# Low-rank products on zero-padded full tiles, among the first heads' values; the input normalised by 512 columns

## The chip, the cores and the metric

The kernel runs on one NeuronCore of one Trainium2 chip. The metric is the device time of one execution in microseconds (us), lower is better. Before the change three runs gave 1459.98, 1460.8 and 1462.34 us; their median is 1460.8 us. One further execution was profiled.

The engines of the core are named as in the profile: PE is TensorE (matrix products and transposes), PEld its weight loads, DVE is VectorE, ACT is ScalarE, POOL is GpSimd, SP issues most of the loads. Each engine works through its own list of instructions in order, and waits where an operand, a buffer or a weight is not ready.

## The reference, cut to what matters

One decoder layer on 272 tokens (16 meta tokens and 256 of the input) of width 2048, in float32:

```python
h = layer_norm(concat([meta, x]), emb_ln_g, emb_ln_b)        # 272 x 2048
p = h @ w_in                                                 # all projections at once
p = p + (p_prev - p) * mu                                    # RWKV columns: shift by one token
r, k, v, wl, al, gl = split(p)                               # 1024, 1024, 1024, 64, 64, 160
w_log = -softplus(-(w0 + tanh(wl) @ w2)) - 0.5               # low rank, 64 -> 1024
a = sigmoid(a0 + al @ a2)                                    # low rank, 64 -> 1024
g = sigmoid(gl) @ g2
... RWKV-7 recurrence per head of 64, stick-breaking attention per head of 64,
... output projection, layer norm, gated MLP of width 5632 with a width-3 convolution, layer norm
```

## The kernel before, in words

**Arithmetic.** A float32 operand is split in two float32r halves, high and low, and a product of two split operands is three PE passes: high x high, high x low, low x high (`passes`, lines 226 to 230, and `each_pass`, lines 493 to 500, in the same order). The tokens are the moving operand (272 or 260 columns), 128 rows of weights are the stationary one. Projecting 2048 input features to 128 output features of one kind for one pair of heads is 16 blocks of the contraction (`KT`) times 3 passes, 48 passes.

**Weights.** `weight(i)` (lines 161 to 189) issues the load of piece i and of a few ahead on SP's queue. ACT copies the piece to the high half (`whi`, or `xhi` for the first 12 pieces), DVE subtracts to get the low half (`wlo`, `xlo`; POOL does it for the first three pieces). The first 12 pieces hold the columns of the low-rank inputs wl, al and gl in blocks of four `KT` steps. Pieces 12 and 13 are k of the first pair of heads, 14 and 15 its v, 16 and 17 its r, and so on. There are three buffers for raw pieces and three for split ones, so a split waits until PE has used an older piece.

**Prologue (lines 306 to 445).** While the input arrives, PE runs 30 idle products (`WARM`). The 272 rows of the input come as three tiles: 16 meta rows, and twice 128 rows. Their means and variances are taken; then a loop (lines 358 to 366) normalises all 2048 columns, in four slices of 512, on DVE (the 16 rows and the second 128 rows) and on ACT (the first 128 rows). Behind it stand a copy of constants and four small DVE operations on the parameters (`omu`, `ngn`, `nsb`, `omka`, lines 367 to 376). `feature_major(kt)` (lines 378 to 387) then transposes 128 columns of all three tiles on PE into one PSUM bank of four, and ACT and DVE turn that into the high and low halves of `ht[kt]`; the low half's subtraction is POOL's for odd `kt`. The loop over `kt` (lines 390 to 398) keeps `LEAD` = 2 such steps ahead, and does 9 passes each for the three groups of low-rank columns (`acc[0]` to `acc[2]`).

**Low rank (lines 400 to 443).** `lora()` shifts the three results by a token, applies tanh and splits into `sh` and `sl`; then for each of the 8 pairs of heads and each of the two matrices (w2, a2) there are two products into one bank: line 432 on all 128 rows (the high half on 64 rows, the low half of the weights against it on the other 64), and line 433 on 64 rows (high half of the weights against the low half `sl`). ACT takes the sigmoid into `sg[j]`. These run as a job beside the projection of k of the first pair (`proj(12, acc[3])`).

**Order.** Up to there a planner with a cost model orders every engine's instructions. From line 453 on, PE's order is the written one. `weave(project(...))` emits the projections pass by pass, and after every 16 passes (`SLOT`) a slot in which waiting tasks put their own products. For the first pair: v, then `rwkv_front(0)` is already begun with k, then r, then `rwkv_back(0)` is begun, then k of the second pair, and so on. `rwkv_front` (lines 575 to 610) makes a cumulative sum of `sg` (line 580), exponentials, and the square of k, and two slots later has PE sum the squares by head (`by_head`, lines 550 to 553, tile `ss`); from it come the tiles `AG` and `BK`. `rwkv_back` (lines 622 to 677) multiplies with r, and two slots later has PE form the sum named `bonus` (line 639, also through lines 552 and 553). The tiles of this stage take the memory of the prologue's, so the first ones wait for the low-rank products.

The rest (the recurrence's chain, attention, output projection, MLP) is not touched.

## Time and profile before

| | us |
|---|---|
| median of three runs | 1460.8 |
| the profiled execution | 1463.17 |
| its span from first to last instruction | 1461.4 |
| PE busy | 1359.3 (93%) |
| DVE busy | 925.5 (63%) |
| ACT busy | 723.9 (50%) |
| POOL busy | 238.9 (16%) |
| mean granted clock of PE | 0.959 |

Busy time is the time in which an engine had an instruction under way; PE's passes overlap, so the pace of a stretch is read from the starts of its passes. A granted clock of 1.00 is 2.4 GHz, of 0.50 is 1.2 GHz. Times of rows count from the start of the span.

### The profile page before, as it was taken

Reading aid. Unit: us, or ns where it says so; the run is one execution under the profiler, and the core shown is the slowest. Engines: PE = TensorE matmul, PEld = TensorE weight load, DVE = VectorE, ACT = ScalarE, POOL = GpSimd, SP = SyncE. Lnnn points to the kernel's source line nnn. Section 1 sums busy time; section 2 is a strip of 40 time slices with the busy share of each in tenths; the row PEclk is TensorE's granted clock in tenths of the full one; section 3 lists DMA queues with packets and bytes.
Section 4 is the critical chain, followed back from the end, with each engine's and each line's share of the span. In section 5 each row is a group of like instructions: output and inputs, shape, how many; then the busy total and the mean of one; then the engine's idle time right before and its main releaser. Section 6 shows DMA issues by size and latency. Waiting matters only on the chain.

```text
span 1461.4 us, 26242 instructions
## 1 busy us (share of the span) xinstructions
PE 1359.3 (93%) x10528; PEld 1267.0 (87%) x10528; DVE 925.5 (63%) x1501; ACT 723.9 (50%) x1227; POOL 238.9 (16%) x417
## 2 busy tenths in 40 slices
PE   7997898778889989897999999999999999999996
PEld 5897887677888888896899999999999998888896
DVE  7477767667867776787965555555555554444445
ACT  6654565436655664544754444444444443333331
POOL 3103664017126000064300000000000000000002
PEclk8798899879999999999999999999999999999998
DMA  7344454223444323554356556655665666666563
GB/s 232 92 127 136 107 155 106 75 70 107 125 128 107 110 84 108 150 159 145 116 183 197 183 179 187 185 186 176 187 186 180 182 187 239 193 192 196 177 199 100
DMA packets 67706, 224.10 MB, mean 153 GB/s; under 512 B 9196, under 2 KB 10932, under 8 KB 67440
## 3 DMA queue, kind: packets, MB, share of 16 engines
q1 hardware_dynamic: 63392, 215.03, 47.5%
q0 software_dynamic: 3328, 4.25, 2.2%
q10 hardware_dynamic: 864, 3.15, 0.5%
q8 instruction: 82, 1.34, 0.4%
q14 instruction: 40, 0.33, 0.1%
HBM read 219.01 MB, written 3.30 MB: 152 GB/s over the span
## 4 chain that ended last, share of the span: by engine, by line
PE 66%; DVE 10%; issue 3%; ACT 3%; DMA 2%; POOL 2%; POOLq 0%; DVEq 0%; ACTq 0%
PE u L230 11%; PE u L228 11%; PE u L229 11%; PE d L1159 5%; PE d L1158 5%; PE d L1160 5%; DVE wlo L187 3%; PE S L495 2%; PE S L499 2%; PE S L497 2%; ACT whi L184 1%; DMA dy<-Y 1%; POOL ytmp L686 1%; POOL Y L688 1%; DMA wraw<-in_w_up_dram 1%
## 5 line engine op out<-in xcount | busy, mean ns | idle before, releaser
L187 DVE TENSOR_TENSOR wlo<-wraw,whi 128x1024 fp32r<-128x1024 f32 (+1 forms) x396 | 484.8, 1230 | 371.9 <-ACT whi L184 365.5
L184 ACT CAST whi<-wraw 128x1024 fp32r<-128x1024 f32 (+1 forms) x396 | 409.1, 1040 | 505.6 <-DMA wraw<-in_w_up_dram 136.7
L228 PE MATMUL u<-h1hi,whi 128*128 128x258 f32 (+2 forms) x1408 | 400.7, 285 | 3.3 <-ACT whi L184 3.3
L230 PE MATMUL u<-h1hi,wlo 128*128 128x258 f32 (+2 forms) x1408 | 398.6, 284 | 3.3 <-DVE wlo L187 3.3
L229 PE MATMUL u<-h1lo,whi 128*128 128x258 f32 (+2 forms) x1408 | 398.6, 283 | 0.0
L230 PEld LDWEIGHTS u<-h1hi,wlo 128*128 128x128 f32 x1408 | 267.9, 190 | 4.4 <-DVE wlo L187 4.4
L228 PEld LDWEIGHTS u<-h1hi,whi 128*128 128x128 f32 x1408 | 267.8, 190 | 4.2 <-ACT whi L184 4.2
L229 PEld LDWEIGHTS u<-h1lo,whi 128*128 128x128 f32 x1408 | 267.6, 190 | 0.0
L1159 PE MATMUL d<-wlo,ahi 128*128 128x512 f32 (+1 forms) x396 | 145.7, 368 | 0.0
L1158 PE MATMUL d<-whi,ahi 128*128 128x512 f32 (+1 forms) x396 | 145.7, 368 | 0.0
L1160 PE MATMUL d<-whi,alo 128*128 128x512 f32 (+1 forms) x396 | 145.3, 367 | 0.0
L495 PE MATMUL S<-h,whi 128*128 128x272 f32 (+1 forms) x384 | 116.2, 303 | 4.0 <-DVE shr L270 2.6
L1173 POOL TENSOR_TENSOR drs<-drs,mhalf 128x1 f32<-128x1 f32 x2 | 2.1, 1036 | 717.1 <-DVE drs L1172 717.1
L499 PE MATMUL S<-h,wlo 128*128 128x272 f32 (+1 forms) x384 | 116.5, 303 | 0.0
L497 PE MATMUL S<-h,whi 128*128 128x272 f32 (+1 forms) x384 | 116.0, 302 | 0.0
L495 PE MATMUL R<-h,whi 128*128 128x272 f32 (+1 forms) x368 | 112.9, 307 | 0.0
L499 PE MATMUL R<-h,wlo 128*128 128x272 f32 (+1 forms) x368 | 112.8, 306 | 0.0
L497 PE MATMUL R<-h,whi 128*128 128x272 f32 (+1 forms) x368 | 112.0, 304 | 0.0
L1158 PEld LDWEIGHTS d<-whi,ahi 128*128 128x128 f32 x396 | 74.5, 188 | 13.1
L1160 PEld LDWEIGHTS d<-whi,alo 128*128 128x128 f32 x396 | 74.5, 188 | 13.0
L1159 PEld LDWEIGHTS d<-wlo,ahi 128*128 128x128 f32 x396 | 74.6, 188 | 12.7
L495 PEld LDWEIGHTS S<-h,whi 128*128 128x128 f32 x384 | 76.5, 199 | 6.1 <-issue 2.9
(384 smaller groups left out, 2284.7 us busy)
## 6 DMA issues: line engine op xcount, KB each, us to landing
wraw<-in_w_up_dram SPq DMA_DIRECT2D x176, 512.0 KB, 3.7
wraw<-in_w_in_dram SPq DMA_DIRECT2D x96, 512.0 KB, 3.5
wraw<-in_w_down_dram SPq DMA_DIRECT2D x88, 512.0 KB, 4.2
wraw<-in_w_out_dram SPq DMA_DIRECT2D x28, 512.0 KB, 3.5
xraw<-in_w_in_dram SPq DMA_DIRECT2D x12, 256.0 KB, 3.7
xt<-in_xin_dram SPq DMA_DIRECT2D x8, 256.0 KB, 5.1
wraw<-in_w_out_dram SPq DMA_DIRECT2D x8, 256.0 KB, 2.6
l<-in_ln_dram ACTq DMA_DIRECT2D x1, 2048.0 KB, 8.3
```

Of the source, the lines that this page charges most:

```text
L184: S.copy(hi[:, :wide], raw[:, :wide])
L187: V.tensor_sub(lo[:, :wide], raw[:, :wide], hi[:, :wide].bitcast(F32))
L228: mm(ps, lhsT=hi[:, sl], rhs=xh, start=start, stop=False)
L229: mm(ps, lhsT=hi[:, sl], rhs=xl, start=False, stop=False)
L230: mm(ps, lhsT=lo[:, sl], rhs=xh, start=False, stop=stop)
L495: mm(ps, lhsT=hi[:, sl], rhs=xh, start=start, stop=False)
L497: mm(ps, lhsT=hi[:, sl], rhs=xl, start=False, stop=False)
L499: mm(ps, lhsT=lo[:, sl], rhs=xh, start=False, stop=stop)
L686: G.tensor_tensor(out=tmp[:n_, :n, :m], in0=Y[:n_, :n, s:s + 1].to_broadcast([n_, n, m]), in1=LT[:n_, s:s + 1, s + 1:].to_broadcast([n_, n ...
L1158: mm(ps, lhsT=ahi[:, f, t_], rhs=hi[:, w], start=f == 0, stop=False)
L1159: mm(ps, lhsT=ahi[:, f, t_], rhs=lo[:, w], start=False, stop=False)
L1160: mm(ps, lhsT=alo[:, f, t_], rhs=hi[:, w], start=False, stop=f == NF - 1)
```

## The change: what it does

Low rank: `sl` becomes two tiles, each zero on the 64 rows it doesn't use, and the second product of each pair of products runs on all 128 rows. The whole of k's first half is put into the last eight steps of the loop over `kt`, its second half behind the loop. PE's written order begins there; v of the first pair is projected in this stage too, and after every 6 of its passes comes one pair of heads' low-rank products (4 of them). v leaves the woven stage, so the woven stage begins with r. Input: the normalisation is a function called for 512 columns at a time, followed by the transposes of these columns (4 `kt`), and then by their products. The copy of constants and the small operations on parameters come behind the loop. 42 idle products in place of 30.

```diff
--- before.py
+++ after.py
@@ -38,8 +38,7 @@
 MEAN = 8
 LATER = 8
 AHEAD = 300
-WARM = 30
-LEAD = 2
+WARM = 42
 CUTS = (0, 512), (512, 1088), (1088, 1664), (1664, 2048)
 LN2 = float(np.log(2.0))
 LEX, KEX = -20, 16
@@ -280,29 +279,8 @@
                     yield
 
 
...
     sg = []
+    order = ctx.enter_context(ExitStack())
     with ExitStack() as es:
         xp = pool(es, "xp")
         xw = pool(es, "xw")
@@ -311,9 +289,10 @@
         acc = [pst.tile([P, 512], F32, tag="acc", bufs=4, name=f"acc{m}") for m in range(4)]
         warm = pst.tile([P, 512], F32, tag="tr", bufs=4, name="warm")
 
-        sl = xp.tile([P, T], F32R, name="sl")
-        V.memset(sl.bitcast(F32), 0.0)
-        idle = sl.bitcast(mybir.dt.bfloat16)[:, :512]
+        sl = [xp.tile([P, T], F32R, name=f"sl{n}") for n in range(2)]
+        for t in sl:
+            V.memset(t.bitcast(F32), 0.0)
+        idle = sl[0].bitcast(mybir.dt.bfloat16)[:, :512]
         for _ in range(WARM):
             mm(warm, lhsT=idle[:, :P], rhs=idle, start=True, stop=True)
 
@@ -355,7 +334,7 @@
                 G.tensor_tensor(out=mr[:r], in0=mv[:r, 0:1], in1=rs[:r], op=ALU.mult)
                 G.tensor_scalar(out=mr[:r], in0=mr[:r], scalar1=-1.0, scalar2=None, op0=ALU.mult)
             norm.append((mv, rs, mr))
-        for k in range(4):
+        def normalise(k):
             c = slice(k * 512, k * 512 + 512)
             for (xt, r, a), (mv, rs, mr) in zip(xs, norm):
                 if a:
@@ -364,16 +343,6 @@
                                         op0=ALU.subtract, op1=ALU.mult)
                 else:
                     S.activation(xt[:r, c], xt[:r, c], AF.Identity, scale=rs[:r], bias=mr[:r])
-        S.copy(trbd, trbd_s)
-
-        omu = ap_.tile([P, 27], F32, name="omu")
-        o = PV["mu_r"][0]
-        V.tensor_scalar(out=omu, in0=pv[:, o:o + 27], scalar1=-1.0, scalar2=1.0, op0=ALU.mult, op1=ALU.add)
-        ngn, nsb = [ap_.tile([P, 8], F32, name=n) for n in ("ngn", "nsb")]
-        for t, n in ((ngn, "gn_g"), (nsb, "sb_g")):
-            V.tensor_scalar(out=t, in0=pars(n), scalar1=-1.0, scalar2=None, op0=ALU.mult)
-        omka = ap_.tile([P, 8], F32, name="omka")
-        V.tensor_scalar(out=omka, in0=pars("k_a"), scalar1=-1.0, scalar2=1.0, op0=ALU.mult, op1=ALU.add)
 
         def feature_major(kt):
             ps = pst.tile([P, 512], F32, tag="tr", bufs=4, name=f"tr{kt}")
@@ -387,15 +356,27 @@
             e.tensor_tensor(out=ht[kt][:, 1], in0=tmp, in1=ht[kt][:, 0].bitcast(F32), op=ALU.subtract)
 
 
-        for kt in range(LEAD):
-            feature_major(kt)
         for kt in range(KT):
-            if kt + LEAD < KT:
-                feature_major(kt + LEAD)
+            if kt % 4 == 0:
+                normalise(kt // 4)
+                for k in range(4):
+                    feature_major(kt + k)
             for m in range(3):
                 hi, lo = weight(kt // 4 * 3 + m, ahead=3)
                 n0 = 12 if m else 0
                 passes(acc[m][:, n0:T], hi, lo, kt % 4, ht[kt][:, 0, n0:], ht[kt][:, 1, n0:], kt == 0, kt == KT - 1)
+            if kt >= 8:
+                passes(acc[3][:, :T], *weight(12, ahead=0), kt - 8, ht[kt - 8][:, 0], ht[kt - 8][:, 1], kt == 8, False)
+        S.copy(trbd, trbd_s)
+
+        omu = ap_.tile([P, 27], F32, name="omu")
+        o = PV["mu_r"][0]
+        V.tensor_scalar(out=omu, in0=pv[:, o:o + 27], scalar1=-1.0, scalar2=1.0, op0=ALU.mult, op1=ALU.add)
+        ngn, nsb = [ap_.tile([P, 8], F32, name=n) for n in ("ngn", "nsb")]
+        for t, n in ((ngn, "gn_g"), (nsb, "sb_g")):
+            V.tensor_scalar(out=t, in0=pars(n), scalar1=-1.0, scalar2=None, op0=ALU.mult)
+        omka = ap_.tile([P, 8], F32, name="omka")
+        V.tensor_scalar(out=omka, in0=pars("k_a"), scalar1=-1.0, scalar2=1.0, op0=ALU.mult, op1=ALU.add)
 
         half = [slice(0, 64), slice(64, 128)]
         weight(11, ahead=0)
@@ -414,7 +395,7 @@
             sh = [tp_.tile([P, T], F32R, tag="tmp", bufs=2, name=f"sh{n}") for n in range(2)]
             for n, (h, o) in enumerate(zip(half, half[::-1])):
                 S.copy(sh[n][h], lw[0][h])
-                V.tensor_sub(sl[h], lw[0][h], sh[n][h].bitcast(F32))
+                V.tensor_sub(sl[n][h], lw[0][h], sh[n][h].bitcast(F32))
                 S.copy(sh[n][o], lw[0][h])
             yield
             for m in (1, 2):
@@ -430,28 +411,31 @@
                     ps = pst.tile([P, 512], F32, tag="tr", bufs=4, name=f"lora{j}{n}")
                     w = w2a2_r[:, n, j * P:j * P + P]
                     mm(ps[:, :T], lhsT=w, rhs=sh[n], start=True, stop=False)
-                    mm(ps[:, :T], lhsT=w[half[n]], rhs=sl[half[n]], start=False, stop=True)
+                    mm(ps[:, :T], lhsT=w, rhs=sl[n], start=False, stop=True)
                     S.activation(t[:, n, PAD:], ps[:, :T], AF.Sigmoid, bias=par(name, j))
                 sg.append(t)
-                if j % 2:
-                    yield
-
-        weight(12)
-        start(lora(), 1)
-        run(proj(12, acc[3]))
-        while jobs:
-            advance()
+                yield
+
+
+        order.enter_context(tc.manual_schedule(engines={PE.engine}))
+        low = lora()
+        next(low)
+        for kt in range(8, KT):
+            passes(acc[3][:, :T], *weight(13), kt - 8, ht[kt][:, 0], ht[kt][:, 1], False, kt == KT - 1)
         shift(acc[3], 8, k_[:, PAD:])
+
+        val = pst.tile([P, 512], F32, tag="acc", bufs=4, name="acc4")
+        for n, _ in enumerate(proj(14, val)):
+            next(low, None)
+        for _ in low:
+            pass
+        shift(val, 16, v_[:, PAD:])
         tc.keep_in_program_order(nc.scalar.preload_act_table_set("natural_log_exp_and_others"))
 
 
     pp = pool(astack, "pp", space=PSUM)
     ap2 = pool(astack, "ap2")
     dp = pool(astack, "dp", space=bass.MemoryType.DRAM)
-
-    order = ctx.enter_context(ExitStack())
-    order.enter_context(tc.manual_schedule(engines={PE.engine}))
-
 
 
 
@@ -878,13 +862,13 @@
     def bank(name):
         return pp.tile([P, 512], F32, tag="proj", bufs=2, name=name)
 
-    piece = 14
+    piece = 16
     state = [dict() for _ in range(NPAIR)]
     for kind, j in ORDER:
         st = state[j]
         if kind == "R":
             for n, dst in ((1, k_), (2, v_), (0, r_)):
-                if n != 1 or j:
+                if n == 0 or j:
                     ps = bank(f"R{j}{n}")
                     weave(project(piece, ps, 12 if n == 0 else 0))
                     piece += 2
```

## Rows read from the trace of the kernel before

**Rows 1.** The profile's first part (busy by engine), and one group of its fifth.
```profile
PE 1359.3 (93%) x10528; PEld 1267.0 (87%) x10528; DVE 925.5 (63%) x1501; ACT 723.9 (50%) x1227; POOL 238.9 (16%) x417
...
L187 DVE TENSOR_TENSOR wlo<-wraw,whi 128x1024 fp32r<-128x1024 f32 (+1 forms) x396 | 484.8, 1230 | 371.9 <-ACT whi L184 365.5
```

**Rows 2.** Stretches: length, busy time (instructions) by engine, granted clock, DMA share, GB/s.
```profile
10.00:20.00 10.00, 3.78 (x15) 2.41 (x15) 9.44 (x18) 6.87 (x12) 7.46 (x9) 0.72 0.61 200
20.00:30.00 10.00, 9.59 (x57) 8.62 (x58) 7.72 (x16) 5.43 (x10) 2.47 (x3) 0.76 0.74 242
...
49.00:67.40 18.40, 18.38 (x58) 12.34 (x58) 2.42 (x4) 10.11 (x22) 0.00 (x0) 0.68 0.11 36
...
60.00:70.00 10.00, 10.00 (x29) 7.07 (x30) 2.28 (x3) 5.81 (x11) 2.30 (x5) 0.50 0.00 0
```

**Rows 3.** Timeline of PE, prologue: start, length, line, operands, count [idle before].
```profile
1.20 8.13 PE L318 MATMUL warm<-sl 128*128 128x512 bf16 x30 [1.20 <-DVE sl L315]
...
20.37 0.90 PE L381 MATMUL tr<-cc,xt 16*128 16x16 f32 x3 [3.24 <-DVE tmp L384]
21.32 0.59 PE L229 MATMUL acc<-h,xhi 128*128 128x272 f32 x1
```

**Rows 4.** Timeline of DVE, then of POOL, same stretch.
```profile
13.24 5.23 DVE L363 TENSOR_SCALAR xt<-xt,mv,rs 128x512 f32<-128x512 f32 x7 [0.48 <-POOL rs L353]
...
19.77 0.54 DVE L384 TENSOR_SCALAR tmp<-tr,pv 128x272 f32<-128x272 f32 x1
...
14.61 5.00 POOL L179 TENSOR_TENSOR xlo<-xraw,xhi 128x512 fp32r<-128x512 f32 x3 [1.40 <-ACT xhi L178]
```

**Rows 5.** Groups of DVE, 13.2 to 47 us: count, busy, mean ns, idle before.
```profile
L384 DVE TENSOR_SCALAR tmp<-tr,pv 128x272 f32<-128x272 f32 x16 | 8.4, 550 | 2.6 <-ACT h L382 2.6
L179 DVE TENSOR_TENSOR xlo<-xraw,xhi 128x512 fp32r<-128x512 f32 x9 | 6.0, 693 | 0.7 <-ACT xhi L178 0.7
```

**Rows 6.** Timeline of PE at full clock: one step's transposes, and six passes apart.
```profile
31.73 0.60 PE L381 MATMUL tr<-cc,xt 16*128 16x16 f32 x3
32.08 0.37 PE L229 MATMUL acc<-h,xhi 128*128 128x272 f32 x1
...
47.88 0.29 PE L228 MATMUL acc<-h,whi 128*128 128x272 f32 x1
...
48.63 0.29 PE L228 MATMUL acc<-h,whi 128*128 128x272 f32 x1
```

**Rows 7.** Timeline of PE at full clock, low-rank products between passes of k.
```profile
57.13 0.39 PE L228 MATMUL acc<-h,whi 128*128 128x272 f32 x1
57.35 0.28 PE L432 MATMUL lora<-sh,w2a_r 128*128 128x272 f32 x1
57.57 0.39 PE L433 MATMUL lora<-sl,w2a_r 64*128 64x272 f32 x1
57.89 0.39 PE L229 MATMUL acc<-h,whi 128*128 128x272 f32 x1
```

**Rows 8.** Timeline of PE: v begins; two passes at half clock; r begins; bonus.
```profile
67.40 0.59 PE L495 MATMUL R<-h,whi 128*128 128x272 f32 x1
...
68.25 0.43 PE L495 MATMUL R<-h,whi 128*128 128x272 f32 x1
68.47 0.43 PE L497 MATMUL R<-h,whi 128*128 128x272 f32 x1
...
76.08 0.28 PE L495 MATMUL R<-h,whi 128*128 128x260 f32 x1
...
87.96 0.39 PE L552 MATMUL bonus<-ss,trbd 128*128 128x258 f32 x1 [1.92 <-ACT ss L546]
88.99 0.39 PE L553 MATMUL bonus<-sq,trbd 128*128 128x258 f32 x1 [0.65 <-DVE sq L547]
```

**Rows 9.** Timeline of DVE; then a stretch from the squares' sum to bonus.
```profile
71.30 0.46 DVE L547 TENSOR_TENSOR ss<-sq,rn 128x288 fp32r<-128x288 f32 x1 [1.45 <-ACT rn L546]
...
74.20:88.94 14.74, 12.22 (x98) 11.80 (x96) 12.34 (x22) 6.57 (x10) 0.00 (x0) 1.00 0.46 142
```

More of the change, by code (lines that the diff above doesn't have):

```diff
@@ L280, in proj @@
                     yield
-    jobs = []
-    def start(gen, wait=0, then=None):
-        jobs.append([wait, gen, then])
-    def advance():
-        for job in list(jobs):
-            if job[0]:
-                job[0] -= 1
-                continue
-            try:
-                next(job[1])
-            except StopIteration:
-                jobs.remove(job)
-                if job[2]:
-                    job[2]()
-    def run(gen):
-        for _ in gen:
-            advance()
     sg = []
+    order = ctx.enter_context(ExitStack())
     with ExitStack() as es:
@@ L432, in lora @@
                     mm(ps[:, :T], lhsT=w, rhs=sh[n], start=True, stop=False)
-                    mm(ps[:, :T], lhsT=w[half[n]], rhs=sl[half[n]], start=False, stop=True)
+                    mm(ps[:, :T], lhsT=w, rhs=sl[n], start=False, stop=True)
                     S.activation(t[:, n, PAD:], ps[:, :T], AF.Sigmoid, bias=par(name, j))
                 sg.append(t)
-                if j % 2:
-                    yield
-        weight(12)
-        start(lora(), 1)
-        run(proj(12, acc[3]))
-        while jobs:
-            advance()
-        shift(acc[3], 8, k_[:, PAD:])
+                yield
[4 more added lines that the diff above has]
+            passes(acc[3][:, :T], *weight(13), kt - 8, ht[kt][:, 0], ht[kt][:, 1], False, kt == KT - 1)
+        shift(acc[3], 8, k_[:, PAD:])
+        val = pst.tile([P, 512], F32, tag="acc", bufs=4, name="acc4")
[4 more added lines that the diff above has]
+        shift(val, 16, v_[:, PAD:])
         tc.keep_in_program_order(nc.scalar.preload_act_table_set("natural_log_exp_and_others"))
```

## The prediction

> **What bounds the kernel now.** I read the busy times first: PE has 93% of the span, no other engine more than 63% [rows 1]. So the end moves with PE, and a change in the first 90 us is worth what it takes from PE's list there, since all that follows is emitted in the same order as before. Then I read the stretches of 10 us for places where PE is idle or at a low clock. There are two. From 10 to 20 us PE is busy for 3.78 us, and the granted clock has a mean of 0.72, then 0.76 up to 30 us, while DVE is busy for 9.44 us: DVE is the bound there. From 49.0 to 67.4 us PE is always busy, but with only 58 instructions in 18.4 us; the clock has a mean of 0.68, and from 60 to 70 it is 0.50, the lower of its two levels (1.2 GHz) [rows 2]. The timelines say why. PE stops at 9.3 us, when its idle products end, and the first low-half pass starts at 21.32; the wait just ahead of it is on a DVE operation of line 384 [rows 3]. DVE couldn't do that one before 19.77, because the remaining normalising operations (seven in 5.23 us from 13.24) and the small operations on parameters stood ahead of it [rows 4].
>
> **The pace of a pass.** At full clock six passes lie between 47.88 and 48.63, 0.125 us each, and the three transposes of one step take 0.35 us (31.73 to 32.08) [rows 6]. At half clock a pass takes 0.22 us (68.25 to 68.47) [rows 8].
>
> **Part 1, the loop over `kt`.** Before, at 49.02 us, PE had done the 144 passes of the loop and 22 passes of k (48 less the 26 that the groups of the stretch from 49.0 still hold: 58 instructions less 32 low-rank ones [rows 2]). With two more, 49.3 us is what compares with the end of the new loop, which holds 144 passes and 24 of k. In the new loop DVE normalises one slice of each tile, and the first transposes follow at about 13.9 as before; but line 384 can follow them at once, not at 19.77. The work that moves costs what it did, and runs beside PE's passes. What paces the loop then? A group of four steps has on DVE 2 normalising operations at 0.75 (5.23/7 [rows 4]), 4 of line 384 at 0.55, 3 low halves of weights at 0.69 [rows 5], and two subtractions no longer than line 384's: 1.5 + 2.2 + 2.1 + 0.9 = 6.7 us. PE has 36 passes and 4 steps of transposes, 4.5 + 1.4 = 5.9 us, in the two groups without k, and 6.0 + 1.4 = 7.4 in the two with it. So DVE paces the first two groups and PE the last two: 13.24 + 2 x 6.7 + 2 x 7.4 = 41.4, and 2 us for waits at the edges of the groups, where all four transposes stand ahead of the passes: 43.5 us. Bounds: if PE has finished the first group and the second's transposes at 20 us (POOL's low halves, 14.61 to 19.61 [rows 4], allow no earlier end of it), 132 passes and 8 steps remain, 16.5 + 2.8, and the loop ends at 39.3; if DVE's order gives all back, at 49.3. I take 43.5: **5.8 us gained**, between 0 and 10.
>
> The 12 more idle products (8.13/30 = 0.27 each [rows 3]) end at 12.6, ahead of the first transposes; they cost nothing unless the input comes over 1 us earlier. They stand in the place of an idle stretch of PE after which the clock was at half. SP's loads keep their order (piece 12 is asked for earlier in the text, but still after piece 11).
>
> **Part 2, the low-rank stage.** At full clock, three instructions (a pass of k, the 128-row product, the 64-row product) take 57.13 to 57.89 = 0.76 us, where three passes in a row take 0.375 [rows 6, 7]. The two switches, to 64 rows and back, thus cost 0.385 us per pair of products, 6.2 us for 16. Of the 18.4 us of the stretch 58 x 0.125 = 7.25 are plain pace, 6.2 the switches, and the remaining 5 the half clock; and v's first passes run at half clock as well (22 of them, some 2.2 us [rows 8]). On full tiles a product is a pass like any other. After the new loop come 24 passes of k, 48 of v and 32 products: 104 x 0.125 = 13.0 us, and 0.5 for a first low-rank product that waits for tanh and the splitting (30 passes, 3.75 us, cover that; without them the wait would be all of it). Before, from 49.3 to the end of v at 76.08 [rows 8], 26.8 us went by. **13.3 us gained.** Bounds: 7.1 if a padded product still costs what the pair did (6.2 less), 13.8 without the wait. The sigmoids on ACT run beside 1.25 us of passes per pair of heads.
>
> The Trainium skill, TensorE: Matmul & The Clock Gate, section Why this matters for your kernels, says that a product with a short contraction takes the same time as a full one, and that the gain lies in running several at once. Taken alone it gives the padding nothing, and the sum is then 6.2 us smaller. The rows on 64-row products differ from that: the start after one comes 0.32 us later (57.57 to 57.89), after a full pass 0.125 [rows 6, 7]. I go by the rows.
>
> **Part 3, what is late next.** v's 48 passes lay between `rwkv_front(0)` and `rwkv_back(0)` and gave DVE and ACT time for the front. They are gone from there, and so PE comes to `bonus` earlier, relative to the front. Before, 76.08 to 88.99 = 12.9 us lay between the start of r and bonus' second product, the last of them a wait [rows 8]. After: the front can begin at the end of the low-rank products (its tiles lie in their memory). In the trace the squares' low half was ready 71.30 + 0.46 - 67.40 = 4.4 us after that point [rows 8, 9]; with the product itself 5.0. From there to bonus DVE's list took 14.74 us [rows 9]. In it were five low halves of weights at 1.2 (mean in [rows 1]) and v's shift, 0.5; with half as many passes beside it, three of the five fall out: 14.7 - 3.6 - 0.5 = 10.6. Together 15.6 us, against PE's own list of 48 + 32 + 2 passes, 10.2 us: PE waits over 5 us at bonus, where it now waits some 3. Also, r may start in the PSUM bank in which v stood and wait a microsecond for v's shift; that wait lies inside the 15.6. Bounds: 10.2, if DVE's order favours the chain, and 21.6 (67.40 to 88.99), if nothing gets shorter. **2.7 us lost.**
>
> **The sum.** 5.8 + 13.3 - 2.7 = 16.4 us less: bonus at 72.6 instead of 88.99. Behind it PE's order, the weights and the slots are the same (48 passes are three whole slots), so the shift stays. The profiled execution gives 1463.2 - 16.4 = 1446.8; it lies 2.4 above the median of the runs, so the median becomes **1444.4 us**.
>
> **Rivals.**
> - *Padding saves the clock, not the switches.* The price of a low-rank pair stays 0.385 us more: 1450.6 us. For it: the skill's sentence above. Against it: rows 7. Chance 0.08.
> - *The low-rank stage stays at half clock,* for a reason other than the 64-row products. For it: the clock was at half for most of the 18.4 us though PE was always busy. Against it: plain passes just ahead ran at 0.125. 80 instructions x 0.1 = 8 us: 1452.4. Chance 0.06.
> - *DVE gives it back.* The loop ends at 49.3 and the front takes its 21.6: 16.4 - 5.8 - 6.0 = 4.6 gained, 1456.2. For it: DVE was busy for 9.4 of 10 us [rows 2], and keeps all its work. Chance 0.06.
> - *The grouped transposes let the clock fall in the loop: slower.* Four steps of transposes in a row, and a wait behind them at each edge of a group, replace single steps between passes. If the clock then stays at half over the loop, 168 passes at 0.22 and 16 steps at 0.7 make 48 us, from about 14.5 to 63, 20 us more than forecast: 1464. It decides when over four fifths of the loop run at half clock. For it: between 10 and 30 us, with transposes and few passes, the clock was at half for about 10 us (means 0.72 and 0.76 [rows 2]). Against it: PE was then idle, and in the loop 36 or 48 passes follow every group. Chance 0.06.
>
> The Trainium skill, TensorE: Matmul & The Clock Gate, Part 4: PE-mode transpose, says that transposes don't count as busy for the clock in the way that products do. That is the rule behind the fourth rival; by it the sum would be 1464. The trace so far doesn't settle it, since transposes and idle time came together.
>
> **How the numbers follow.** The forecast's own case (a loop that ends between 39 and 47 us, a front between 11 and 18) has 0.70 and gives 1438 to 1451. With the first two rivals 0.84 lies up to 1454; so the range is 1438 to 1454. The remaining 0.04 is no visible change (a different planning of ACT and DVE in the woven stage that costs what the start gains). A change of under 0.2%, 2.9 us, can't be told from none. Faster: forecast and first three rivals, less a little, 0.88; same 0.05; slower 0.07.
>
> **What would show it.** Right: the loop's last pass at about 43.5; low-rank products 0.125 us apart with a granted clock of 1.00; r's first pass near 57; a longer wait at bonus, whose second product stands near 72.6; and the same distance from there to the end as before. Wrong: a granted clock of 0.5 in the loop; PE waiting for a low half of weights or of `h` for several us; a wait at bonus beyond 8 us; or a stretch behind 100 us that has become longer.

## The result and the profile after

| | before | after |
|---|---|---|
| median of 12 runs each, us | 1460.4 | 1451.53 |
| ratio, 95% interval | | 0.9944 [0.9926, 0.9961] |
| the profiled execution, us | 1463.17 | 1458.17 |
| its span, us | 1461.4 | 1456.4 |
| mean granted clock | 0.959 | 0.958 |
| PE / DVE busy, us | 1359.3 / 925.5 | 1359.0 / 927.4 |

The change gains 8.9 us of 1460 (by the interval of the ratio, 5.7 to 10.8). The forecast was a gain of 16.4 us (1444.4 us), the range 1438 to 1454. Both the sign and the range hold; about half of the forecast's gain did not come. Three marks on PE's timeline show where:

| mark, us from the span's start | before | forecast | after |
|---|---|---|---|
| loop done (144 passes, and 24 of k) | 49.3 | 43.5 | 47.9 |
| k, v and low-rank products done | 76.1 | 57.0 | 61.4 |
| bonus' second product | 88.99 | 72.6 | 78.93 |

The middle stage is as forecast (13.5 us from 47.9 to 61.4). The loop before it and the front behind it are each too long, by 4.4 and 1.9 us. (The 49.3 of before is the prediction's count and holds the 0.26 us in which the first low-rank product waited. Counted as in the later table, by passes alone, before's loop is done at 49.0; the loop then gains 1.1 us and the stage 13.6.)

The stretches of after, to be read beside [rows 2] (length, busy time of PE, PEld, DVE, ACT and POOL with instructions, granted clock, DMA share, GB/s):

```profile
10.00:20.00 10.00, 7.54 (x30) 4.26 (x27) 9.46 (x18) 7.53 (x14) 7.23 (x9) 0.71 0.55 181
20.00:30.00 10.00, 9.29 (x60) 8.93 (x61) 8.51 (x15) 5.96 (x10) 4.18 (x5) 0.78 0.91 306
...
47.90:61.40 13.50, 13.49 (x106) 13.13 (x104) 6.68 (x11) 12.81 (x30) 0.00 (x0) 1.00 0.35 123
...
61.40:78.90 17.50, 12.35 (x85) 11.77 (x83) 11.15 (x21) 10.34 (x19) 2.30 (x5) 0.90 0.33 102
```

The first two are almost those of before: DVE busy for 9.46 of 10 us, the clock at 0.71 and 0.78. The third holds 106 instructions in 13.5 us at full clock, where before 58 took 18.4.

PE's timeline in the prologue (start, length, line, operands, count, idle before), beside [rows 3]:

```profile
13.36 3.03 PE L350 MATMUL tr<-cc,xt 16*128 16x16 f32 x12 [1.62 <-DVE xt L342]
16.83 1.03 PE L227 MATMUL acc<-h,xhi 128*128 128x272 f32 x3 [0.44 <-ACT h L351]
18.08 1.74 PE L350 MATMUL tr<-cc,xt 16*128 16x16 f32 x6 [0.22 <-DVE tmp L353]
20.71 0.59 PE L228 MATMUL acc<-h,xhi 128*128 128x272 f32 x1 [0.89 <-DVE h L356]
21.10 0.43 PE L229 MATMUL acc<-h,xlo 128*128 128x272 f32 x1
```

The transposes come early and in a group, and still the products that need a low half begin at 20.7. The next groups of transposes on the same timeline show when the first two groups of 36 passes, and the third with its 48, were done:

```profile
26.54 1.13 PE L350 MATMUL tr<-cc,xt 16*128 16x16 f32 x6
...
32.00 2.19 PE L350 MATMUL tr<-cc,xt 16*128 16x16 f32 x12
...
39.99 2.20 PE L350 MATMUL tr<-cc,xt 16*128 16x16 f32 x12
```

DVE and POOL in the first stretch, beside [rows 4]:

```profile
13.79 3.77 DVE L342 TENSOR_SCALAR xt<-xt,mv,rs 128x512 f32<-128x512 f32 x6 [0.48 <-POOL rs L332]
17.48 1.01 DVE L353 TENSOR_SCALAR tmp<-tr,pv 128x272 f32<-128x272 f32 x2
18.42 0.81 DVE L178 TENSOR_TENSOR xlo<-xraw,xhi 128x512 fp32r<-128x512 f32 x1
19.16 1.50 DVE L356 TENSOR_TENSOR h<-tmp,h 128x272 fp32r<-128x272 f32 x1
...
15.34 5.02 POOL L178 TENSOR_TENSOR xlo<-xraw,xhi 128x512 fp32r<-128x512 f32 x3 [1.59 <-ACT xhi L177]
```

DVE still does seven of the eight normalising operations ahead of line 353 (these six, and one at 12.77), though the text calls for two: the planner put the later slices' operations first, as it did before. And the subtraction of line 356 takes 1.50 us, which later in the loop takes 0.43; it ends at 20.66, just behind POOL's three (20.36).

Low-rank products, beside [rows 7], then r's start and bonus, beside [rows 8]:

```profile
52.83 0.29 PE L229 MATMUL acc<-h,wlo 128*128 128x272 f32 x1
52.95 0.29 PE L413 MATMUL lora<-sh,w2a_r 128*128 128x272 f32 x1
53.08 0.29 PE L414 MATMUL lora<-sl,w2a_r 128*128 128x272 f32 x1
...
61.27 0.29 PE L414 MATMUL lora<-sl,w2a_r 128*128 128x272 f32 x1
63.94 0.39 PE L479 MATMUL R<-h,whi 128*128 128x260 f32 x1 [2.38 <-DVE shv L269]
...
69.41 0.29 PE L536 MATMUL ss<-rn,trbd 128*128 128x288 f32 x1
...
78.05 0.39 PE L536 MATMUL bonus<-ss,trbd 128*128 128x258 f32 x1 [2.31 <-ACT ss L530]
78.93 0.57 PE L537 MATMUL bonus<-sq,trbd 128*128 128x258 f32 x1 [0.49 <-DVE sq L531]
```

A padded product starts 0.125 us after the one ahead of it, as a pass does. r's first pass waits 2.38 us for v's shift (line 269), which reads the bank that r is to write.

**Behind bonus.** The first product of the gate (line 777, before line 793) comes at 314.65 instead of 326.98, the first of the MLP (`u`) at 671.82 instead of 678.16. So the gain was still whole at 327 us (12.3); the profiled execution lost 6 us of it between 330 and 680, where its clock was 0.95 and that of before's 0.97:

```profile
330.00:680.00 350.00, 319.41 (x2809) 297.92 (x2807) 264.41 (x516) 199.56 (x410) 97.81 (x158) 0.95 0.41 122
```

It is the slowest of after's 12 runs (1447.46 at a mean clock of 0.970 to 1458.17 at 0.958), 6.6 us over their median. The marks of the first 90 us are therefore a better measure of the change than this one execution's end.

### The profile page after: what moved, and what is told of

It reads as the page before. It is cut to its first block, busy times and chain, and to the rows that moved or that the text cites. A ratio compares the mean times of both kernels' runs of the same rounds, so it can differ in the third digit from the quotient of the medians.

```text
span 1456.4 us, 26271 instructions
## 1 busy us (share of the span) xinstructions
PE 1359.0 (93%) x10540; PEld 1270.7 (87%) x10540; DVE 927.4 (64%) x1502; ACT 724.4 (50%) x1227; POOL 239.1 (16%) x417
## 4 chain that ended last, share of the span: by engine, by line
PE 66%; DVE 10%; issue 3%; ACT 3%; DMA 3%; POOL 2%; POOLq 0%; DVEq 0%; ACTq 0%
PE u L227 11%; PE u L229 11%; PE u L228 11%; PE d L1143 5%; PE d L1142 5%; PE d L1144 5%; DVE wlo L186 3%; PE S L479 2%; PE S L481 2%; PE S L483 2%; ACT whi L183 1%; DMA wraw<-in_w_up_dram 1%; POOL ytmp L670 1%; POOL Y L672 1%; PE R L483 1%
## 5 line engine op out<-in xcount | busy, mean ns | idle before, releaser
L479 PE MATMUL R<-h,whi 128*128 128x272 f32 (+1 forms) x352 | 108.7, 309 | 2.4 <-DVE shv L269 2.4
L483 PE MATMUL R<-h,wlo 128*128 128x272 f32 (+1 forms) x352 | 108.8, 309 | 0.0
L481 PE MATMUL R<-h,whi 128*128 128x272 f32 (+1 forms) x352 | 108.3, 308 | 0.0
L1142 PEld LDWEIGHTS d<-whi,ahi 128*128 128x128 f32 x396 | 74.5, 188 | 13.2
```

Of the source, the lines that this page charges most:

```text
L479: mm(ps, lhsT=hi[:, sl], rhs=xh, start=start, stop=False)
L481: mm(ps, lhsT=hi[:, sl], rhs=xl, start=False, stop=False)
L483: mm(ps, lhsT=lo[:, sl], rhs=xh, start=False, stop=stop)
L1142: mm(ps, lhsT=ahi[:, f, t_], rhs=hi[:, w], start=f == 0, stop=False)
```

## The experiments

Two theories stood at first. One: the padding makes the gain, and the loop and the front lose because of waits that can be named (DVE's order, POOL, the clock; the bank). The other: v's move or the new input makes the gain. Each build has 6 to 12 runs and one trace. The ratios are to runs of before taken beside them, whose medians were 1461.77, 1459.72 and 1460.99 us for the first, second and last four builds, so builds are compared by the ratio. The marks are those of the table above; "loop" counts 144 passes and 24 of k, with 0.125 us for each pass of k that an order puts on the other side.

| run | loop done | last low-rank product | bonus' second | median, us | ratio to before, 95% |
|---|---|---|---|---|---|
| after | 47.9 | 61.3 | 78.9 | 1451.53 | 0.9944 [0.9926, 0.9961] |
| half tiles | 49.1 | 68.0 | 86.0 | 1461.27 | 1.0000 [0.9983, 1.0018] |
| padding alone | 49.7 | 57.4 | 79.5 | 1452.29 | 0.9934 [0.9912, 0.9955] |
| own bank for v | 49.9 | 63.2 | 79.2 | 1454.39 | 0.9947 [0.9925, 0.9969] |
| old input | 50.0 | 63.2 | 80.8 | 1455.38 | 0.9957 [0.9938, 0.9977] |
| slices held back | 50.3 | 63.6 | 81.6 | 1451.97 | 0.9944 [0.9923, 0.9964] |
| v woven | 47.8 | 59.0 | 79.1 | 1454.71 | 0.9950 [0.9930, 0.9971] |
| bank, slices | 48.9 | 62.2 | 78.2 | 1451.10 | 0.9943 [0.9920, 0.9965] |
| v woven, slices | 50.6 | 61.6 | 81.8 | 1456.20 | 0.9975 [0.9952, 0.9998] |
| low halves on DVE | 48.6 | 61.7 | 78.2 | 1453.51 | 0.9960 [0.9933, 0.9986] |
| the same, slices | 47.5 | 61.7 | 79.6 | 1452.90 | 0.9956 [0.9935, 0.9978] |
| filled loop | 48.7 | 61.9 | 77.9 | 1449.99 | 0.9930 [0.9909, 0.9951] |
| all together | 47.1 | 61.3 | 77.2 | 1449.64 | 0.9928 [0.9908, 0.9948] |

Over the 14 kernels (before with them), the time follows bonus' mark: a line through them (times by the ratios) has a slope of 0.90 us per us, with a correlation of 0.89. Most of that rests on before and half tiles; among the other twelve, whose marks span 4.5 us, the correlation is 0.62. So what the start gains, the end keeps in the main; a difference of 1 or 2 us between two builds is not shown by it.

### Half tiles

```diff
-                    mm(ps[:, :T], lhsT=w, rhs=sl[n], start=False, stop=True)
+                    mm(ps[:, :T], lhsT=w[half[n]], rhs=sl[n][half[n]], start=False, stop=True)
```

> The changed kernel with the second low-rank product on 64 rows again. Theory (a switch between 128 and 64 rows costs, and lets the clock fall): the low-rank products are no longer 0.125 us apart, the stage from the first pass of k's second half (47.9 us) to the end of the low-rank products, 13.5 us in the changed kernel, becomes 19.7 us at full clock (16 pairs x 0.385) and up to 25 us with the clock at half; the median rises by 5 to 11 us. Rival (the written order and v's passes between them are what counts): the stage stays at 13.5 to 14.5 us and the time stays.

Without the padding nothing of the gain shows in the time: 1.0000, though bonus still comes 3.0 us earlier than in before, slightly more than the interval leaves room for. PE's timeline of this kernel, four low-rank products between passes:

```profile
54.78 0.29 PE L229 MATMUL acc<-h,wlo 128*128 128x272 f32 x1
54.91 0.29 PE L413 MATMUL lora<-sh,w2a_r 128*128 128x272 f32 x1
55.12 0.39 PE L414 MATMUL lora<-sl,w2a_r 64*128 64x272 f32 x1
55.44 0.39 PE L413 MATMUL lora<-sh,w2a_r 128*128 128x272 f32 x1
55.76 0.39 PE L414 MATMUL lora<-sl,w2a_r 64*128 64x272 f32 x1
```

The starts are 0.21, 0.32 and 0.32 apart instead of 0.125, as in [rows 7]. The stage, 106 instructions again:

```profile
49.10:68.20 19.10, 19.10 (x106) 14.74 (x104) 6.65 (x11) 14.22 (x31) 0.00 (x0) 1.00 0.32 90
```

19.1 us against after's 13.5, at a clock of 1.00: 5.6 us are the switches alone (6.2 in the forecast). With six full passes to every four products, the half clock of [rows 2] did not come back.

### Padding alone

```diff
-        sl = xp.tile([P, T], F32R, name="sl")
+        sl = [xp.tile([P, T], F32R, name=f"sl{n}") for n in range(2)]
...
-                V.tensor_sub(sl[h], lw[0][h], sh[n][h].bitcast(F32))
+                V.tensor_sub(sl[n][h], lw[0][h], sh[n][h].bitcast(F32))
...
-                    mm(ps[:, :T], lhsT=w[half[n]], rhs=sl[half[n]], start=False, stop=True)
+                    mm(ps[:, :T], lhsT=w, rhs=sl[n], start=False, stop=True)
```

(in the kernel before)

> The kernel before with the full tiles alone; order, input and v as before. Theory: the stretch with low-rank products, 18.4 us before, becomes 8 to 9.5 us (58 instructions at 0.125 us and waits for the sigmoids), v's passes run at full clock, bonus' second product comes at 77 to 79 us in place of 88.99, and the median falls by about as much as with the whole change (8 to 11 us). Rival (v beside them and the written order are needed): the stretch still takes over 15 us, the time falls by less than 3 us.

This one edit has the whole gain: 0.9934, and bonus at 79.5 where after has 78.9. The stretch that answers to before's 49.0 to 67.4:

```profile
49.70:57.50 7.80, 7.78 (x59) 7.49 (x60) 2.47 (x5) 7.74 (x19) 0.00 (x0) 1.00 0.28 84
```

About the same instructions (59, before 58) take 7.8 us at full clock instead of 18.4 at 0.68: 10.6 less, where the forecast had 6.2 for switches and 5 for the clock. ACT is busy for 7.74 of the 7.80, and PE's 59 starts at 0.125 make 7.4: both are full, and which of them sets the pace isn't shown. The new input and the move of v together bring nothing that shows in the time.

### Own bank for v

```diff
-        val = pst.tile([P, 512], F32, tag="acc", bufs=4, name="acc4")
+        val = acc[2]
```

> The changed kernel, with v accumulated in the bank of the third low-rank group, which r does not use. Theory: the 2.4 us in which r's first pass waits for v's shift go, and with them the 3.4 us at half clock behind it; the squares' sum is then held by ACT and DVE (ready at 66.5), so bonus' second product comes at 76 to 77 us in place of 78.93 and the median falls by 2 to 3 us. Rival (the front's chain on ACT and DVE from the end of the low-rank products sets bonus whatever PE does): bonus stays within 0.7 us of 78.9 and only the wait at bonus grows.

PE's timeline, from the last low-rank product to r:

```profile
63.22 0.29 PE L414 MATMUL lora<-sl,w2a_r 128*128 128x272 f32 x1
63.34 0.28 PE L479 MATMUL R<-h,whi 128*128 128x260 f32 x1
```

The stretch from there to bonus:

```profile
63.30:79.20 15.90, 11.23 (x86) 10.30 (x84) 11.17 (x21) 10.19 (x20) 2.31 (x5) 0.98 0.39 118
```

r's wait is gone, and bonus comes 15.9 us after the last low-rank product, not 17.5: the bank costs 1.6 us. Bonus still stands where it stood, because the loop of this trace ends 2.0 us later (49.9). That isn't the planner's doing: in after, half tiles, own bank and v woven, PE, DVE, ACT and POOL have the same operations in the same order up to the end of the loop. What differs is the clock, and with the own bank the start too (first low-half pass at 22.28, in after at 21.10). The stretch from 20 to 30 us of half tiles, own bank and v woven, in this order (after's stands above, at 0.78):

```profile
20.00:30.00 10.00, 9.35 (x52) 8.75 (x51) 6.95 (x14) 4.91 (x10) 3.48 (x3) 0.66 0.74 250
20.00:30.00 10.00, 9.35 (x49) 8.22 (x49) 7.18 (x13) 4.75 (x9) 4.48 (x4) 0.64 0.75 258
20.00:30.00 10.00, 9.34 (x62) 8.79 (x62) 8.19 (x15) 6.27 (x11) 4.35 (x4) 0.80 0.86 276
```

The loops end at 49.1, 49.9 and 47.8, after's at 47.9: where the clock has the lower mean, the loop ends later. So the loop's mark in one trace carries 2 us that do not come from the build.

### Old input

```diff
-WARM = 42
+WARM = 30
...
+        for kt in range(2):
+            feature_major(kt)
         for kt in range(KT):
-            if kt % 4 == 0:
-                normalise(kt // 4)
-                for k in range(4):
-                    feature_major(kt + k)
+            if kt + 2 < KT:
+                feature_major(kt + 2)
```

(and the normalising loop and the operations on constants ahead of it, as before; the rest of the change stays)

> The changed kernel with the input's part undone: all four slices normalised and the small operations done ahead of the transposes, two steps of transposes ahead, 30 idle products. Theory (the planner had put nearly all normalising operations first anyway): the first pass of k's second half comes at 49 to 50 us in place of 47.9, the median rises by 1 to 2 us. Rival (the input's part is worth what was forecast): 53 us or later, the median rises by 5 us or more.

The loop ends at 50.0, bonus stands at 80.8: the new input is worth 2 us at these marks, where the forecast had 5.8. The same new input, in the same order, gave ends from 47.8 to 49.9, and here the clock of the stretch from 20 to 30 us has a mean of 0.68, so even the 2 us are not shown; the intervals of the times overlap.

### Slices held back, and with the own bank

```diff
+                if k:
+                    behind = tail[0 if a else 1]
...
-                    with tc.issue_after(last.ins):
+                    with tc.issue_after(behind.ins):
```

(`tail` is the previous slice's last `tmp` on DVE and last high half on ACT)

> The changed kernel with the slices' order forced: on DVE and on ACT the normalising of a slice is queued behind the last step of the slice ahead of it. Theory (the input's part failed because the planner put six of DVE's seven operations and all four of ACT's ahead of the first transposed step): the first DVE operation on a transposed step comes at 15 to 16 us in place of 17.5, the first low-half pass before 19 in place of 21.1, and k's second half begins at 44 to 46 us in place of 47.9 (47.7 to 49.7 over the runs with this loop); the median falls by 2 to 4 us. Rival (POOL's low halves of the first weights, DVE's total work and the half clock after the start hold the loop, whatever the order): k's second half begins at 47.5 or later and the median stays.

Now DVE's six normalising operations are one, and its first `tmp` still stands at 17.63, as in after (17.48). DVE, and POOL beside it:

```profile
13.76 1.48 DVE L346 TENSOR_SCALAR xt<-xt,mv,rs 128x512 f32<-128x512 f32 x1 [0.48 <-POOL rs L332]
15.16 1.24 DVE L383 TENSOR_SCALAR omu<-pv 128x27 f32<-128x27 f32 x1
16.32 0.16 DVE L386 TENSOR_SCALAR ngn<-pv 128x8 f32<-128x8 f32 x1
16.39 1.25 DVE L386 TENSOR_SCALAR nsb<-pv 128x8 f32<-128x8 f32 x1
17.63 1.02 DVE L362 TENSOR_SCALAR tmp<-tr,pv 128x272 f32<-128x272 f32 x2
...
13.66 1.29 POOL L178 TENSOR_TENSOR xlo<-xraw,xhi 128x512 fp32r<-128x512 f32 x1
14.89 1.48 POOL L178 TENSOR_TENSOR xlo<-xraw,xhi 128x512 fp32r<-128x512 f32 x1
16.32 1.28 POOL L178 TENSOR_TENSOR xlo<-xraw,xhi 128x512 fp32r<-128x512 f32 x1
```

`ngn` and `nsb` are the same operation on as many elements and take 0.16 and 1.25 us. The long ones end at 15.24, 16.40 and 17.64; POOL's three end at 14.95, 16.37 and 17.60. So the theory for the last four runs: DVE waits inside its operation until POOL's is over. The Trainium skill, SBUF — State Buffer, section SBUF: two separate sides, says that the two engines share a pair of ports as an exclusive lock: a GpSimd operation, or a DVE operation in a two-port mode or with two SBUF inputs, holds the pair for the whole instruction if it starts first, and the other one blocks. The rows agree, DVE's long operations ending 0.03 to 0.3 us behind POOL's; which mode DVE's were in, no row tells. POOL's own lengths vary too (1.28 to 1.48 us here, up to 1.94 in after), so POOL may be waiting for DVE as well; that was not tried.

The build did what its rival said: the loop ends at 50.3, and the time is after's.

> The changed kernel with forced slices and v in its own bank. If both theories hold: bonus' second product at 73 to 76 us in place of 78.93, the median 3 to 6 us below that of the changed kernel. Rival (DVE and ACT hold the start and the front): bonus not before 78, the median within 2 us of the changed kernel.

Both waits were aimed at, one went: r follows at once (62.36). The loop ends at 48.9, and at 50.3 and 50.6 in the other two builds with the slices held back alone; the three have the same order of operations up to there, and clocks of 0.87, 0.71 and 0.70 from 20 to 30 us. The time is after's.

### v woven, and with held-back slices

```diff
-        for n, _ in enumerate(proj(14, val)):
-            next(low, None)
         for _ in low:
             pass
...
-    piece = 16
+    piece = 14
```

> The changed kernel with v back in the woven stage; the low-rank products run in a row behind k's second half. Theory (v's move gave nothing: PE's work is the same, and v between front and back hides the front's work on ACT and DVE): the low-rank products end at 58 to 59 us (32 of them, paced by 16 sigmoids of 0.43 us), bonus' second product comes at 77 to 79 us, and the median is the same or up to 1.5 us lower. Rival (v among the products pays, since the sigmoids hold them otherwise): bonus at 81 us or later, the median rises by 2 us or more.

> The changed kernel with forced slices and v back in the woven stage. If v's move gives nothing and the slices 2 to 4 us: bonus' second product at 74 to 76 us, the median 2 to 4 us below that of the changed kernel and no worse than with v's own bank. Rival (the slices give nothing): bonus at 77 to 79 us, the median that of the changed kernel.

With v back in the woven stage the low-rank products stand alone and go at ACT's pace, and bonus comes at 79.1, after's 78.9:

```profile
50.84:59.10 8.26, 6.49 (x34) 5.76 (x33) 3.10 (x6) 8.23 (x21) 0.00 (x0) 0.79 0.45 143
```

ACT is busy for 8.23 of 8.26 us, PE for 6.49, at a clock of 0.79. PE's passes of v are not lost behind it: they cover the front. A gain or loss from v's place shows neither at bonus nor in the ratio (0.9950 against 0.9944). The second build's loop ends 2.8 us later, and its bonus comes 2.6 us later, outside of both its theory's and its rival's range.

### Low halves on DVE, and with held-back slices

```diff
-                (G if n < 3 else V).tensor_tensor(out=lo, in0=raw[:, :wide], in1=hi.bitcast(F32), op=ALU.subtract)
+                V.tensor_tensor(out=lo, in0=raw[:, :wide], in1=hi.bitcast(F32), op=ALU.subtract)
```

> The changed kernel, but the low halves of the first three weights are taken by DVE instead of POOL. Theory (DVE stands still while POOL runs its long subtractions): without them DVE's operations of the loop's start keep their usual length (0.53 us for a normalising one, 0.15 for one on a parameter, 0.43 to 0.55 for a low half of h; in the changed kernel some take 1.2 to 1.5), and no DVE operation ends together with a long POOL one. DVE takes on three operations of 0.7 to 1.2 us, so its sum changes little: the first low-half pass between 19 and 21 us (20.71 in the changed kernel), the first pass of k's second half at 46 to 48 (47.93). Rival (DVE's list alone is the bound, POOL does not hold it): the short operations stay as long as before, and the first low-half pass comes 2 to 3 us later. Time 1449 to 1453 by the theory, 1453 to 1456 by the rival.

> The changed kernel with the first three weights' low halves on DVE and the later slices' normalising operations held back behind the slice before. Alone, the held-back slices had left the first write of the loop's line 356 chain at 17.6 us, because DVE's small operations lay beside POOL's long ones. Theory (POOL's operations hold DVE): now both causes are gone, DVE's first tmp operation comes near 16.0 to 16.6 us, the first low-half pass near 18 to 18.5, and the first pass of k's second half at 46 to 47.5 us; the bonus' second product at 77 to 78 instead of 78.93; time 1449 to 1452. Rival (the transposes come too late, or the low halves on DVE now stand ahead of tmp): first low-half pass not ahead of 19.7, first pass of k's second half at 48 or later, no change of the time.

DVE's timeline in the first kernel, without POOL's long operations beside it:

```profile
17.03 0.56 DVE L353 TENSOR_SCALAR tmp<-tr,pv 128x272 f32<-128x272 f32 x1
17.51 0.68 DVE L178 TENSOR_TENSOR xlo<-xraw,xhi 128x512 fp32r<-128x512 f32 x1
18.11 0.43 DVE L356 TENSOR_TENSOR h<-tmp,h 128x272 fp32r<-128x272 f32 x1
```

PE's first low-half pass in the first kernel, and then in the second:

```profile
18.98 0.43 PE L229 MATMUL acc<-h,xlo 128*128 128x272 f32 x1
```

```profile
17.73 0.43 PE L229 MATMUL acc<-h,xlo 128*128 128x272 f32 x1
```

Line 356 takes 0.43 us, not 1.50; the first low-half pass comes 2.1 and 3.4 us earlier than after's 21.10. That POOL's operations hold DVE's is borne out. But the loop ends at 48.6 and 47.5, not 2 to 3 us earlier as its first low-half pass does, and both times lie above the theory's ranges: in the first kernel PE waits 2.0 us for a low half of `h` later on, and in the second the passes run at half clock (0.22 apart) from 17.7 to 23.2 us. In these two builds an earlier first pass did not bring an earlier end.

### Filled loop, and all together

```diff
                     feature_major(kt + k)
+                    for _ in range(0 if kt else 5):
+                        mm(acc[3], lhsT=idle[:, :P], rhs=idle, start=True, stop=True)
```

> The changed kernel with 20 more idle products of 512 columns on TensorE, five behind each of the first four steps of transposes, into a bank that is not in use yet. Nothing is left out. Theory (the half clock from about 12 to 26 us is the price of TensorE's idle time there): with the idle time filled, the granted clock's mean between 20 and 30 us rises from 0.78 to over 0.9, the passes that ran 0.22 apart there run 0.125 apart, and the first pass of k's second half comes 1.5 to 3 us earlier than 47.93, if the idle products (20 at 0.22 to 0.43 us, 4.4 to 8.6 us in all) end before the first low-half pass could start. Rival (the loop is paced by DVE, so the clock is free): first pass of k's second half within 0.5 us of 47.93 though the clock is up. Second rival: the idle products push the transposes and with them the whole loop back by 1 to 3 us. Time 1449 to 1451 by the theory, 1451 to 1454 by the others.

> The changed kernel with all that the other runs point to: the first three weights' low halves on DVE, the later slices' normalising operations held back, 20 more idle products behind the first four steps of transposes, and v in the bank of an accumulator that is free, so that r need not wait for v's shift. If the loop term of the prediction failed for DVE's order, POOL's hold and the half clock together, the first pass of k's second half comes at 44 to 46 us, the bonus' second product at 74 to 76, and the time is 1447 to 1449.5. If these are not the bound, the first is at 47 to 49, the second at 77.5 to 79, and the time is that of the changed kernel, 1450 to 1453.

The idle products hold the clock at 1.00 up to 20 us (0.71 in after); then PE waits 1.5 us for DVE, and it falls to a mean of 0.83 in the next 10 us. The loop ends at 48.7, 0.8 later than after's: nearest to the rival by which the idle products delay it. The time (1449.99) lies where the theory had it, but the mark speaks against the theory. Bonus comes 1.0 us earlier than after's for another reason: in this build r starts at 62.05, directly behind the last low-rank product, without the wait for v's shift (which is at 64.05), and bonus follows 15.8 us behind, as with v's own bank. The edit doesn't touch v's bank; why r and v no longer share one is not known. In the kernel with all edits the clock stays at 1.00. Its loop as a stretch:

```profile
19.00:48.40 29.40, 29.01 (x214) 25.95 (x214) 26.74 (x44) 19.12 (x34) 6.73 (x7) 1.00 0.66 206
```

On its PE timeline a group of transposes:

```profile
32.06 0.28 PE L229 MATMUL acc<-h,xlo 128*128 128x260 f32 x1
32.27 2.19 PE L359 MATMUL tr<-cc,xt 16*128 16x16 f32 x12
34.22 0.37 PE L228 MATMUL acc<-h,whi 128*128 128x272 f32 x1
```

PE is busy for 29.0 of 29.4 us at full clock, with waits of 0.3 us in all, and the loop still ends at 47.1, less than a microsecond earlier than after's. So here PE's own list is the bound, from its first pass on. Four steps of transposes take 1.95 us (32.27 to 34.22), 0.49 a step and not 0.35. From the first pass at 18.5, 168 passes at 0.125 and 12 steps at 0.49 make 45.4; short gaps, most of them at the edges of the transposes, make up the other 1.7. Its last low-rank product ends where after's does: the stage behind the loop waits for `sh` and a sigmoid (0.23 and 0.22 us, with further short gaps), and ACT is busy for 12.3 of its 13.0 us. Bonus at 77.2 is after's less the bank's 1.6; r starts at 61.40. Its time and that of the filled loop are the lowest, but their intervals overlap after's: that they beat it is not shown.

## Why the prediction was right and wrong

**Right: the low-rank stage.** 13.3 us were forecast and 13.3 measured (76.1 - 49.3 = 26.8 before, 61.4 - 47.9 = 13.5 after; 13.6 with before's loop counted by passes alone). The half-tile run prices the switches by themselves: 5.6 us (6.2). Padding alone gives the sum of switches and clock: 10.6 (11.2). The first two rivals fall: the clock was 1.00 through the stage, and a padded product cost 0.125 us. By the Trainium skill, TensorE: Matmul & The Clock Gate, section Why this matters for your kernels, a short contraction takes the same time as a full one, and padding would have brought nothing. The rows of products that alternate with full ones say otherwise (0.32 us from start to start, 0.125 when padded); a row of short ones alone was not run.

**Wrong in size: the loop.** 5.8 us forecast, 1.4 measured. The term that failed is the first group of four steps, 13.24 + 6.7: by it the group's 36 passes are done at 19.9. In after they were done at 26.5, 6.6 us later. The three groups behind it took 5.4, 8.0 and 8.0 us, 21.4 together, where the sum had 6.7, 7.4, 7.4 and 2 for the edges, 23.5. Three things make up the first group's miss.

- "Line 384 can follow them at once": it could by its operands, but the planner put five more normalising operations first.
- DVE's operations were as long as POOL's beside them, which the prediction had read as DVE's own length. The trace of before already had it: behind the rows of [rows 4] the first small operation takes 1.22 us and ends at 19.62, where POOL's three end at 19.61, and the next ones take 0.15:

```profile
18.40 1.22 DVE L371 TENSOR_SCALAR omu<-pv 128x27 f32<-128x27 f32 x1
```

- The term counts DVE's list alone and lets PE end with it, at full clock. PE had 33 passes left behind its first low half, 4.1 us at 0.125, and up to 24.4 us they ran 0.22 apart.

With all three mended (all together) the first group was done at 23.6 and the loop at 47.1; 3.6 of the 4.4 missing microseconds were still missing. A part of these is the price of the idle products, which put the first pass at 18.50, where the build with DVE's order and POOL mended alone had it at 15.18 and its first low-half pass at 17.73; a loop that starts so early at full clock was not run. The sum also priced four steps of transposes at 1.4 us from a single step between passes [rows 6], where a group takes 1.95; this counts only in the last two groups, which PE paces (48 passes and 1.95 make 7.95 of their 8.0), and the 2 us for edges paid for it. The lower bound of 39.3 took PE to have finished the first group by 20 us, and no run came near that: in all of them, the first low-half pass came at 17.7 or later.

**Wrong in size: the front.** 2.7 us lost forecast, 4.6 measured. The wait of r for v's shift was foreseen, and the step said that it "lies inside the 15.6". It does not: the squares' product (`ss`) stands in PE's written order behind passes of r, so the wait delays the head of the chain. With v in another bank, `ss` is done 5.3 us after the last low-rank product, bonus 15.8 to 15.9 us after it, near the forecast's 5.0 + 10.6. With the wait, `ss` is done at 8.3 us, and part of the delay is made good later (17.5). Passes at half clock behind the wait (65.4 to 68.6 us, 0.215 apart) are in that, and seem to be the larger part: the first build with the low halves on DVE has the same wait of r, but the passes behind it run at full clock,

```profile
64.40:68.40 4.00, 4.00 (x33) 4.00 (x34) 1.37 (x3) 3.60 (x8) 0.00 (x0) 1.00 0.56 169
```

and there `ss` is done at 6.8 us and bonus at 16.3. By this one trace the wait alone costs 0.5 of the 1.6 us. Of the wait of over 5 us that was forecast at bonus, after has 2.8 there and 2.4 at r.

**Right in the main: the shift stays.** 1.4 + 13.3 - 4.6 = 10.1, and bonus came 10.06 us earlier; over all kernels 0.90 of each microsecond at bonus is found in the time, with the reserve made above. The third rival (DVE gives it back, 1456.2) had the right signs in both its terms but too large a front; the fourth (grouped transposes keep the clock down) did not come: from 30 us the clock was 1.00, with groups of twelve transposes in it.

**Left open.** Why the clock of loops with the same order of operations comes back at different times: the passes are 0.22 apart up to 24.4 us in after, 26.8 in half tiles, 27.2 with the own bank and 23.9 with v woven. Whether ACT's sigmoids or PE's own list bound the new stage is not separated: in after PE's 106 starts at 0.125 make 13.25 of 13.5 us, and ACT is busy for 12.81; no run took work from either.

## What to carry to other kernels

Products of a shorter contraction among full ones cost switches (here 0.385 us a pair). In the kernel before they also went with the half clock; that their density was the reason is not shown. Zero padding, an edit of a few lines, bought both back. Before a text is reordered to free an engine, look which order its planner will write and which of the long operations are waits in disguise: an operation whose length varies eightfold between equal shapes, and which ends with another engine's, was a wait here. Price a group of instructions from a group, not from one instance that lies between other work, and price the first round of a loop by itself: here it was the one that came 6.6 us late. And before a difference of 2 us between two builds is explained, compare the clock of the stretch.

## What the runs showed of the hardware that was not expected

- DVE's operations on operands in SBUF can stand still while POOL's run: 0.16 us became 1.25 (`ngn`, `nsb`), 0.43 became 1.50 (line 356). Two operations that read PSUM (line 353 in after, 17.48) kept their 0.5 us beside the same POOL operations.
- The same alternation of 64-row and 128-row products that went with a clock of 0.68 in the kernel before ran at 1.00 in the half-tile run, where more full passes lie between (the written order and v's place differ too).
- Runs of one kernel differ by 10 us with the mean granted clock: after's 12 runs go from 1447.46 at 0.970 to 1458.17 at 0.958, with a correlation of -0.92.
- Four builds with the same order of operations up to the end of the loop ended it between 47.8 and 49.9 us; those that ended it at 49.1 and 49.9 had a clock of 0.66 and 0.64 from 20 to 30 us, those that ended it at 47.9 and 47.8 one of 0.78 and 0.80.
